# HGRN2 layer with MLP on one core: the MLP's first 512 hidden columns in seven block products, and half of one head's values kept on the chip

## The chip, the core and the metric

The kernel runs on one core of a Trainium2 chip. TensorE (PE in the profile) multiplies, PEld is its weight load, VectorE (DVE), ScalarE (ACT) and GpSimd (POOL) work on data in SBUF and PSUM, and SyncE (SP) issues most of the DMAs. The metric is the time of one execution on the device in microseconds (us), as a median of runs.

## The reference

One layer on x of 1024 rows (tokens) by 1024 columns, all in float32: a gated linear recurrence (HGRN2, 8 heads of 128), then an MLP with squared ReLU and 4096 hidden columns, each behind an RMS norm and added to x, and a last norm.

```python
h = _rmsnorm(x, norm_mix)
x = x + _hgrn2_mixer(h, w_in, lb, out_norm, w_out)   # q, f, i, g = split(h @ w_in); S_t = diag(f_t) S_{t-1} + k_t v_t^T
...                                                  # o = S_t^T q_t, normed, times silu(g), then o @ w_out
h = _rmsnorm(x, norm_mlp)
a = jax.nn.relu(h @ w1)                              # 1024x1024 by 1024x4096
x = x + (a * a) @ w2                                 # 1024x4096 by 4096x1024
return _rmsnorm(x, norm_final)
```

## The kernel before

**A product in three.** A float32 product is made of three matmuls in a faster format (fp32r). Each operand is split into a high part, a copy in that format that ACT makes (`AF.Copy`), and a low part, the rest, which DVE makes by a subtraction. `split_mm` (L222 to L225) then issues high by high, high by low and low by high. So each operand costs one pass of ACT and one of DVE.

**Seven products for eight.** Large products are done on 2 x 2 blocks with seven block products instead of eight (Winograd's form of Strassen's method). In the MLP a unit is 512 of the 4096 hidden columns; there are eight units. The blocks of the first product's activations are B11, B21 (first half of the 1024 rows) and B12, B22 (second half); their sums are t1 to t4. A unit's weights are four blocks a, b, c, d and the sums s1 to s4. The order of the seven (`SEQ`) is a on B11, s1 on t1, s2 on t2, s4 on B22, s3 on t3, b on B21, d on t4. Each is 24 matmuls of 128x512 into two PSUM banks of one of three sets (X, Y, Z); a set collects several block products, and `evac_1` moves what is needed into SBUF, adds, and applies ReLU and square.

**The stages in the trace.** Up to 424 us the heads' projections and scans; 424 to 528 the output projection (`proj_out`, PSUM name `op`), first for columns 0 to 511, then for 512 to 1023, with the scan of the last head (7) issued in units between its matmuls until about 466; from 528 the MLP's first product, unit 0 until 579, units 1 to 7 until about 820; then its second product and the last norm.

**Unit 0 before.** Unit 0 alone is a plain product, eight block products of 24 matmuls, 192 (`plain_mm`, PSUM names `pl`). x after the mixer is normed by row blocks of 128 (`hm`, `hn`, by `norm_scale`), transposed on PE eight times for each half of the rows (L206, PSUM name `tr`), copied with the norm's gain into `V` by ACT (L883), and split (`h1B`, L885 to L888). `transposes_2` makes such steps as a list of hooks; hooks of half 0 run in the output projection, those of half 1 between the matmuls of unit 0. `block_sums` (L96 to L104) later makes t1 to t4 out of `V`, in place, and `split_sum` (L115, L116) splits them into `ht`, for units 1 to 7.

**The order.** PE's order is written out by hand everywhere. In the output projection's second half and behind it, that of ACT, DVE, POOL and SP is the program's too; in the head stage these four are placed by a scheduler in order of priority. On each engine and queue instructions run in order, so what waits holds up what stands behind it.

**Values of the heads.** `zt` (L712 to L722) makes a head's output values, transposed, in two halves of 512 rows: DVE multiplies into `sg` (L718) and SP stores each half into `z_d` in DRAM (L721); only head 7's stay. `fetch` (L741) loads them again (`iz`, L747), and `split_value` (L736 to L738) splits them into `zh` for the output projection; in the same way it loads and splits the projection's weights (`iw` into `wo`). The table `LEFT` says which loads go with which block product of the last head; with its third last product, s3, goes head 6's first half, alone:

```python
LEFT = {"b": ("z", 0, range(last - 1), ("m0", "m1", "m8")), "s2": ("w", 0, range(4), ("hT07", "m9")),
        "s1": ("w", 0, range(4, last), ("m10", "m11")), "s3": ("z", 0, range(last - 1, last), ("m0",))}
```

In the scan of the last head, L397 and L403 make k and f for the next level, L390 q, L584 `qe`, and L590, L608 and L638 are PE's small matmuls for these levels (`lv`), whose results L568 to L572 copy under masks into `Ac`. L156 is the helper for additions, which adds the projection's result to x (`xr`) among others; L903 and its like store x into DRAM (`xd`).

Of the kernel before, what the change touches and what calls it, by code (L numbers as in the profile page):

```python
# [29 lines left out]
P = 128  # L30
D = 1024
# [18 lines left out]
def trunk(ctx: ExitStack, tc: tile.TileContext, x, gains, masks, gfin, w_in, w_out, w1, w2, out):  # L50
# [44 lines left out]
    def block_sums():  # L95

        for k in range(2):
            nc.vector.tensor_tensor(R[0, k], R[0, k], R[1, k], ALU.subtract)
        for k in range(2):
            nc.vector.tensor_tensor(R[1, k], R[1, 2 + k], R[1, k], ALU.subtract)  # L100
        for k in range(2):
            nc.vector.scalar_tensor_tensor(R[1, 2 + k], R[0, k], -1.0, R[1, 2 + k], op0=ALU.mult, op1=ALU.subtract)
        for k in range(2):
            nc.vector.scalar_tensor_tensor(R[0, 2 + k], R[1, 2 + k], -1.0, R[0, 2 + k], op0=ALU.mult, op1=ALU.subtract)  # L104

    def split_sum(n):
        half, k0 = SUMS[n]
# [155 lines left out]
    with tc.tile_pool(name="scan", bufs=1) as sp:  # L263
# [277 lines left out]
        def scan_units(h, tl):  # L541
# [168 lines left out]
            def zt():  # L710

                z = tl["sg"]  # L712
                for a in range(2):
# [6 lines left out]
                    if h < NH - 1:  # L720
                        nc.sync.dma_start(z_d[h][:, o], z[:, o])  # L721
# [18 lines left out]
        def fetch(what, half, heads_, places):  # L740

            for h0, m in zip(heads_[::2], places):
# [11 lines left out]
                "s1": ("w", 0, range(4, last), ("m10", "m11")), "s3": ("z", 0, range(last - 1, last), ("m0",))}  # L754
# [79 lines left out]
    def raw_tile(name):  # L834

        k = raw_no[0] % 9
        raw_no[0] += 1
        if k < 2:
            return mslot(k, [P, D], name)
        return slot((12, 13, 14, 8, 9, 10, 11)[k - 2], [P, D], name)  # L840
# [29 lines left out]
    load_w1(0, "abcd")  # L870
    hm = [slot(tb, [P, D], f"hm{tb}") for tb in range(4)]
    rs = {}
    junk = slot(14, [P, D], "junk")
    w0 = {}

    def transposes_2(half, hn):

        def one(kb):
            flat, g, t = transposed(1, half, kb, hn)
            if kb % 2 == 0:  # L880
                R[half, kb // 2] = slot((4, 8)[half] + kb // 2, [P, 2, 512], f"V{half}{kb}")
            r = R[half, kb // 2][:, kb % 2]
            nc.scalar.activation(r, flat, AF.Copy, scale=g)  # L883
            if kb % 2:
                nc.scalar.activation(t[:, 0], r, AF.Copy)  # L885
            else:
                nc.vector.tensor_copy(t[:, 0], r)
            nc.vector.tensor_tensor(t[:, 1], r, t[:, 0].bitcast(F32), ALU.subtract)  # L888
        return [lambda kb=kb: one(kb) for kb in range(KB)]

    def norm_first(tb):
        nc.sync.dma_start(x1[tb], xs[tb])
        rs[tb] = norm_stats(xs[tb], 8 + tb, hm[tb])
        if tb in (1, 2):
            norm_scale(hm[tb - 1], xs[tb - 1], rs[tb - 1], True)
        if tb == 3:
            norm_scale(hm[2], xs[2], rs[2])
            w0["a"] = split_w(raw["a", 0], "wa0")
            norm_scale(hm[3], xs[3], rs[3])
            w0["b"] = split_w(raw["b", 0], "wb0")  # L900

    def norm_second(tb):
        nc.sync.dma_start(x1[tb], xs[tb])  # L903
        rs[tb] = norm_stats(xs[tb], 8 + tb, junk)
        for _ in range((0, 2, 3, 3)[tb - 4]):
            hook()

    order_all(E.SP)
    proj_out(A, 1, range(NH), norm_first)
    hooks += transposes_2(0, hm)  # L910
    proj_out(B, 1, range(NH), norm_second)
    while hooks:
        hook()
    hn = [slot(tb - 4, [P, D], f"hn{tb}") for tb in B]
    for tb in B:
        norm_scale(hn[tb - 4], xs[tb], rs[tb], tb % 2)


    def act_tile(n, u):
        return slot({"e11": u % 2, "e22": 2, "e12": 3, "e21": 4 if u else 13, "t1": 5, "t2": 6, "t4": 7}[n], [P, 2, 512], f"{n}{u}")  # L920

    def square(t):
        nc.scalar.activation(t, t, AF.Square)  # L923

    def relu_square(t, sign=1.0):
        nc.scalar.activation(t, t, AF.Relu, scale=sign)  # L926
        square(t)

    def store(n, u, t):
        nc.sync.dma_start(act_d[n, u], t)  # L930

    def combos_1(u, e):

        t1 = e["t1"] = act_tile("t1", u)
        nc.vector.tensor_tensor(t1, e["e11"], e["e12"], ALU.subtract)
        store("t1", u, t1)
        nc.vector.tensor_tensor(e["e12"], e["e22"], e["e12"], ALU.subtract)
        store("t3", u, e["e12"])
        t2 = e["t2"] = act_tile("t2", u)
        nc.vector.scalar_tensor_tensor(t2, t1, -1.0, e["e22"], op0=ALU.mult, op1=ALU.subtract)  # L940
        store("t2", u, t2)

    def combos_2(u, e):
        t4 = act_tile("t4", u)
        nc.vector.scalar_tensor_tensor(t4, e["t2"], -1.0, e["e21"], op0=ALU.mult, op1=ALU.subtract)
        store("t4", u, t4)

    def plain_mm(i, half):

        pss = [psum.tile([P, 512], F32, name=f"pl{i}{half}{p}", tag="d") for p in range(2)]  # L950
        for k in range(2):
            w = w0["abcd"[2 * i + k]]
            for p in range(2):
                for kb in range(4):
                    o = slice((4 * p + kb) * P, (4 * p + kb + 1) * P)
                    t = hc[("B11", "B21", "B12", "B22")[2 * half + k], kb]
                    if k:
                        hook()
                    split_mm(pss[p], w[0][:, o], w[1][:, o], t[:, 0], t[:, 1], (k, kb) == (0, 0), (k, kb) == (1, 3))
        return pss  # L960

    def plain_out(e, n, pss):
        t = e[n] = act_tile(n, 0)
        for p in range(2):
            nc.scalar.activation(t[:, p], pss[p], AF.Relu)
        square(t)

    e0 = {}
    hooks += transposes_2(1, hn)
    w0["c"] = split_w(raw["c", 0], "wc0")  # L970
    hooks.insert(4, lambda: w0.update(d=split_w(raw["d", 0], "wd0")))
    c11 = plain_mm(0, 0)
    while hooks:
        hook()
    plain_out(e0, "e11", c11)
    c21 = plain_mm(1, 0)
    load_w1(1, "acdb")
    block_sums()
    plain_out(e0, "e21", c21)
    c12 = plain_mm(0, 1)  # L980
    c22 = plain_mm(1, 1)
    split_sum("t3")
    split_sum("t1")
    split_sum("t2")
# [5 lines left out]
    first_2 = (NU - 1) * NS  # L990
# [38 lines left out]

    prep(0)  # L1030
    plain_out(e0, "e12", c12)
    prep(1)
    prep(2)
    plain_out(e0, "e22", c22)
    split_sum("t4")
    for n in ("e11", "e21", "e22"):
        store("B" + n[1:], 0, e0[n])

    def evac_1(u, m, e, ps):
# [6 lines left out]
        elif m == "d":  # L1046
            t = e["e21"] = act_tile("e21", u)
            for p in range(2):
                nc.scalar.activation(t[:, p], ps[p], AF.Relu, scale=-1.0)
            square(t)  # L1050
            store("B21", u, t)
            combos_1(u, e)
            combos_2(u, e)
        else:
            t = e[{"s4": "e12", "s3": "e22", "b": "e11"}[m]]
            for p in range(2):
                nc.vector.tensor_tensor(t[:, p], t[:, p], ps[p], ALU.add)  # L1057
            relu_square(t, -1.0 if m == "s3" else 1.0)
            if m == "s3":
                store("B22", u, t)  # L1060
            if m == "b":
                store("B11", u, t)
# [51 lines left out]
    def product_2(k, pb, s, first, last_):  # L1114
        hi, lo = sides[k]
        w = ws[k]
        for p in range(2):
            o, t = slice(512 * p, 512 * p + 512), slice(P * pb, P * pb + P)
            split_mm(banks[s][pb], hi[:, p, t], lo[:, p, t], w[0][:, o], w[1][:, o], first and p == 0,
                     last_ and p == 1, skip_group_check=True)  # L1120

    banks, e = {}, {}
    for k, (which, u, v, s, m, n) in enumerate(steps):
        first = m in ("a", "s1", "b")
        ending = which == 2 and u >= 4
        if first and v == 0:
            banks[s] = [psum.tile([P, 512], F32, name=f"m{which}{s}{u}{p}", tag=BANK[s]) for p in range(2 * which)]
        load_act(k + LOOK + 2)
        if which == 1:
            w = ws.pop(k)  # L1130
            for p in range(2):
                for kb in range(4):
                    o = slice((4 * p + kb) * P, (4 * p + kb + 1) * P)
                    t = hc[n, kb]
                    split_mm(banks[s][p], w[0][:, o], w[1][:, o], t[:, 0], t[:, 1], first and kb == 0, kb == 3,
                             skip_group_check=True)
            if u + 1 < NU and m in ("s2", "s4"):
# [84 lines left out]
```

## Time and profile before

| | |
|---|---|
| median of 3 runs | 1156.57 us (1155.76 to 1157.57) |
| the profiled execution | 1156.81 us |
| its span, first to last instruction | 1155.0 us |
| granted PE clock, mean | 0.998 of full speed |
| PE busy | 1138.8 us, 99%, 7106 instructions |
| DVE busy | 789.9 us, 68%, 1140 |
| ACT busy | 577.7 us, 50%, 1008 |

Busy times are of the profiled execution. PE's is near the span, so the kernel's time is the work that PE is given and the few microseconds in which PE waits. A row of a timeline has the start and the duration in us, then engine, line, operation and tiles (output, then inputs), and in brackets how long the engine was idle before and what released it. Neighbouring rows on PE overlap, since matmuls are pipelined.

### The profile page before, as it was taken

What the parts mean: (1) busy time and instruction counts of PE and PEld (TensorE: products, weight loads), DVE (VectorE), ACT (ScalarE), POOL (GpSimd) and SP (SyncE); (2) the same over time, 40 slices, a digit from 0 to 9 for tenths busy, and PEclk for the clock granted to TensorE, in tenths of its full rate; (3) what the DMA queues carried; (4) which work ended last, traced back from release to release, by engine and by line L of the source; (5) the groups of instructions that cost most, each with busy time, mean ns of one, the idle gap of its engine ahead of it and who ended that gap; (6) DMA issues with size and microseconds to landing.
All of it is one profiled execution on the core that took longest, in us unless ns stands there. A gap on an engine that the chain in (4) does not pass through costs nothing.

```text
span 1155.0 us, 17539 instructions
## 1 busy us (share of the span) xinstructions
PE 1138.8 (99%) x7106; PEld 941.4 (82%) x7106; DVE 789.9 (68%) x1140; ACT 577.7 (50%) x1008; POOL 38.6 (3%) x67
## 2 busy tenths in 40 slices
PE   8999999999999999999999999999999999999997
PEld 7778888787878878888888888888888888888886
DVE  6997878768687775436756654665487756677673
ACT  7656556474655663237544554454453443323552
POOL 1000000000000000010000000000000000000011
PEclk9999999999999999999999999999999999999999
DMA  7112111111121274121245324542797545322331
GB/s 260 37 38 74 56 37 56 56 38 56 57 64 47 83 264 129 37 91 55 91 164 201 147 90 164 200 163 84 278 368 288 191 159 191 137 91 92 128 128 74
DMA packets 43138, 143.38 MB, mean 124 GB/s; under 512 B 4912, under 2 KB 5040, under 8 KB 43056
## 3 DMA queue, kind: packets, MB, share of 16 engines
q1 hardware_dynamic: 42192, 141.05, 34.5%
q8 instruction: 56, 0.92, 0.3%
q10 hardware_dynamic: 864, 1.20, 0.3%
q14 instruction: 26, 0.21, 0.1%
HBM read 100.81 MB, written 41.42 MB: 123 GB/s over the span
## 4 chain that ended last, share of the span: by engine, by line
PE 87%; DVE 8%; ACT 2%; DMA 1%; issue 1%; POOL 0%; SPq 0%; POOLq 0%; DVEq 0%; ACTq 0%
PE m2X L224 5%; PE m2X L223 5%; PE m2X L225 5%; PE m1X L225 4%; PE m1X L223 4%; PE m1X L224 4%; PE pX L223 3%; PE pX L225 3%; PE pX L224 3%; PE m2Y L224 3%; PE m2Y L225 3%; PE m2Y L223 3%; PE op L223 2%; PE op L225 2%; PE op L224 2%; PE m1Y L225 2%
## 5 line engine op out<-in xcount | busy, mean ns | idle before, releaser
L1023 ACT ACTIVATE a<-ai 128x1024 fp32r<-128x1024 f32 x56 | 59.0, 1053 | 71.5 <-PE m2X L224 24.5
L1024 DVE TENSOR_TENSOR a<-ai,a 128x1024 fp32r<-128x1024 f32 x56 | 68.2, 1218 | 11.5 <-ACT a L1023 11.5
L926 ACT ACTIVATE e<-e 128x1024 f32<-128x1024 f32 x21 | 22.3, 1062 | 67.3 <-DVE e L1057 67.3
L223 PE MATMUL op<-wo,zh 128*128 128x512 f32 x128 | 51.0, 399 | 0.0
L225 PE MATMUL op<-wo,zh 128*128 128x512 f32 x128 | 50.0, 391 | 0.0
L224 PE MATMUL op<-wo,zh 128*128 128x512 f32 x128 | 49.8, 389 | 0.0
L156 DVE TENSOR_TENSOR xr<-xr,op 128x512 f32<-128x512 f32 x24 | 16.4, 686 | 44.9 <-PE op L225 44.9
L1084 DVE TENSOR_TENSOR acc<-acc,m2X 128x512 f32<-128x512 f32 x32 | 21.1, 684 | 35.7 <-PE m2X L225 35.6
L390 DVE TENSOR_TENSOR q<-q,f 128x512 f32<-128x512 f32 x56 | 38.4, 686 | 2.1 <-PE lv L638 2.0
L397 DVE TENSOR_TENSOR k<-k,f 128x512 f32<-128x512 f32 x56 | 38.2, 683 | 0.0
L923 ACT ACTIVATE e<-e 128x1024 f32<-128x1024 f32 x32 | 34.0, 1062 | 1.0
L615 ACT ACTIVATE AT<-Ac 32x256 f32<-32x256 f32 x32 | 13.3, 415 | 37.8 <-DVE Ac L611 32.8
L156 DVE TENSOR_TENSOR raw<-raw,raw 128x512 f32<-128x512 f32 x42 | 28.9, 687 | 0.8
L225 PEld LDWEIGHTS op<-wo,zh 128*128 128x128 f32 x128 | 24.0, 188 | 5.2
L224 PEld LDWEIGHTS op<-wo,zh 128*128 128x128 f32 x128 | 24.1, 188 | 4.7
L223 PEld LDWEIGHTS op<-wo,zh 128*128 128x128 f32 x128 | 24.0, 188 | 4.8
L1045 ACT ACTIVATE e<-m1X 128x512 f32<-128x512 f32 x28 | 16.0, 592 | 19.9 <-PE m1X L225 19.9
L707 ACT ACTIVATE z<-o,rs_z 128x128 f32<-128x128 f32 x64 | 17.4, 384 | 16.3 <-POOL rs_z L126 16.3
L695 PE MATMUL o<-v,AT 128*128 128x128 f32 x128 | 23.4, 275 | 0.0
L697 PE MATMUL o<-S,q 128*128 128x128 f32 x112 | 21.7, 275 | 0.0
L1084 DVE TENSOR_TENSOR acc<-acc,m2Y 128x512 f32<-128x512 f32 x16 | 10.8, 685 | 15.4 <-PE m2Y L225 13.2
L125 POOL TENSOR_SCALAR rs_f<-fs 128x1 f32<-128x1 f32 x4 | 2.0, 512 | 577.7 <-ACT ot L1088 577.7
(1726 smaller groups left out, 3712.9 us busy)
## 6 DMA issues: line engine op xcount, KB each, us to landing
raw<-in_w_in SPq DMA_DIRECT2D x32, 512.0 KB, 3.7
ai<-adt SPq DMA_DIRECT2D x32, 512.0 KB, 4.5
adB<-e SPq DMA_DIRECT2D x24, 512.0 KB, 2.6
adt<-t SPq DMA_DIRECT2D x24, 512.0 KB, 4.3
ai<-adB SPq DMA_DIRECT2D x24, 512.0 KB, 4.5
x<-in_x SPq DMA_DIRECT2D x8, 512.0 KB, 7.2
iw<-in_w_out SPq DMA_DIRECT2D x16, 256.0 KB, 3.4
xr<-in_x SPq DMA_DIRECT2D x8, 512.0 KB, 6.7
```

The source lines that it names most:

```text
L156: nc.vector.tensor_tensor(out_, a, b, ALU.add)
L223: nc.tensor.matmul(ps, lhi, rhi, start=start, stop=False, **more)
L224: nc.tensor.matmul(ps, lhi, rlo, start=False, stop=False, **more)
L225: nc.tensor.matmul(ps, llo, rhi, start=False, stop=stop, **more)
L390: nc.vector.tensor_tensor(qo, qo, te.to_broadcast([P, n, m]), ALU.mult)
L397: nc.vector.tensor_tensor(ke, ke, to.to_broadcast([P, n, m]), ALU.mult)
L695: nc.tensor.matmul(ps[:, j, :], AT[:, c, :], v[:, c, :], start=True, stop=c == 0)
L923: nc.scalar.activation(t, t, AF.Square)
L926: nc.scalar.activation(t, t, AF.Relu, scale=sign)
L1023: nc.scalar.activation(hi, x, AF.Copy)
L1024: nc.vector.tensor_tensor(lo, x, hi.bitcast(F32), ALU.subtract)
L1084: nc.vector.tensor_tensor(t, t, ps, op)
```

## The change

Two things are changed.

**Unit 0 in seven block products.** `plain_mm`, `plain_out` and `block_sums` go; unit 0 joins the list of steps of units 1 to 7 with an order of its own: a on B11, b on B21, s1 on t1, s2 on t2, s3 on t3, s4 on B22, then unit 1's a, then d on t4. It has 168 matmuls. Its weights need seven splits and four sums, made by `prep`, which stands partly in the norm stage; t1 to t4 are made one by one by `sums`, the transposes of half 1 run in the last part of the first block product and in the second, and the splits of B22 come behind the third, those of B12 go. What follows each product on ACT, DVE and SP is listed in `behind_0`. Unit 1's weights are loaded at other points, the places of raw weights are given by a new table, and unit 0's results go through copies and additions out of PSUM, as those of the other units, in place of a ReLU straight out of PSUM.

**Head 6, first half.** Its values are split where `zt` makes them; the store into DRAM, the load, and the entry "s3" of `LEFT` go. The second half of head 6 is stored and loaded as before.

```diff
-    def block_sums():
...
+    def split_sum(n, at=None):
+        half, k0 = at or SUMS[n]
...
-                    if h < NH - 1:
+                    if (h, a) == (last - 1, 0):
+                        t = zh[0, h] = place("z", 0, h)
+                        split_value(t, z[:, o])
+                    elif h < last:
                         nc.sync.dma_start(z_d[h][:, o], z[:, o])
...
-                "s1": ("w", 0, range(4, last), ("m10", "m11")), "s3": ("z", 0, range(last - 1, last), ("m0",))}
+                "s1": ("w", 0, range(4, last), ("m10", "m11"))}
...
-        k = raw_no[0] % 9
+        k = raw_no[0]
         raw_no[0] += 1
...
+        place = ("m0", "m1", 12, 13, 14, "m0", 10, 11, 8, 9)[k] if k < 10 \
+            else ("m1", 13, "m0", 10, 9, 12, 14, 11, 8)[(k - 10) % 9]
...
-    def plain_mm(i, half):
...
-    c11 = plain_mm(0, 0)
...
-    plain_out(e0, "e11", c11)
-    c21 = plain_mm(1, 0)
-    load_w1(1, "acdb")
-    block_sums()
...
     steps = [(1, u, 0, *s) for u in range(1, NU) for s in SEQ]
+    steps[:1] = [(1, 0, 0, *SEQ[i]) for i in (0, 5, 1, 2, 4, 3)] + [steps[0], (1, 0, 0, *SEQ[6])]
...
+    def split_block(half, kb):
+        name = BLOCKS[half][kb // 4]
+        r = R[half, kb // 2][:, kb % 2]
+        t = hc[name, kb % 4] = hslot(half, kb, f"h1{name}{kb}")
+        if half or kb % 2:
+            nc.scalar.activation(t[:, 0], r, AF.Copy)
+        else:
+            nc.vector.tensor_copy(t[:, 0], r)
+        nc.vector.tensor_tensor(t[:, 1], r, t[:, 0].bitcast(F32), ALU.subtract)
+
+    def sums(n, ks=range(2)):
+        for k in ks:
+            a, b, c, d = R[0, k], R[0, 2 + k], R[1, k], R[1, 2 + k]
+            if n == "t1":
+                nc.vector.tensor_tensor(a, a, c, ALU.subtract)
...
+        if tb == 3:
+            norm_scale(hm[2], xs[2], rs[2])
+            prep(0)
+            norm_scale(hm[3], xs[3], rs[3])
+            prep(1)
...
+        if tb == 4:
+            prep(2)
+        for _ in range((3, 3, 2, 0)[tb - 4]):
+            hook()
+        if tb == 7:
+            prep(3)
...
+        if tb == 7:
+            prep(4)
+            load_w1(1, "a")
...
+    def adds_1(m, e, ps):
+        t = e[ADDED[m]]
+        for p in range(2):
+            nc.vector.tensor_tensor(t[:, p], t[:, p], ps[p], ALU.add)
...
+    behind_0 = {
+        1: (lambda: sums("t2"), split_5, lambda: evac_0("a"), lambda: split_sum("t2", t1_at)),
+        2: (lambda: sums("t3"), lambda: split_sum("t3")),
+        3: (lambda: copy_0(0), lambda: [split_block(1, kb) for kb in range(4, 8)], lambda: copy_0(1), lambda: evac_0("s1")),
+        4: (lambda: prep(6), lambda: sums("t4"), lambda: split_sum("t4")),
...
+    hooks += [lambda: None] + tr[:4] + [lambda: (sums("t1", (0,)), block_sum(raw, "s4", 0), sums("t1", (1,)), tr[4]()), tr[5], lambda: (split_sum("t1"), tr[6]()), tr[7]]
     for k, (which, u, v, s, m, n) in enumerate(steps):
...
+                    if k == 1 or (k, p) == (0, 1) and kb > 1:
+                        hook()
```

What moves is shown by the engines' orders; line numbers of the changed file are 11 lower up to L718 (now L707) and 8 lower behind it (L738 is L730). DVE where head 6's values are made, before: the two halves of the values, `sg6`, between weight splits.

```order
L738 TENSOR_TENSOR wo02_4433<-iw02_4430,wo02_4433 128x512
L718 SCALAR_TENSOR_TENSOR sg6_3904<-zt60_4406,gz_166,sg6_3904 128x512
L718 SCALAR_TENSOR_TENSOR sg6_3904<-zt61_4413,gz_166,sg6_3904 128x512
L738 TENSOR_TENSOR wo00_4424<-iw00_4421,wo00_4424 128x512
L738 TENSOR_TENSOR wo01_4427<-iw00_4421,wo01_4427 128x512
```

Changed:

```order
L707 SCALAR_TENSOR_TENSOR sg6_3904<-zt60_4406,gz_166,sg6_3904 128x512
L707 SCALAR_TENSOR_TENSOR sg6_3904<-zt61_4415,gz_166,sg6_3904 128x512
L730 TENSOR_TENSOR wo00_4426<-iw00_4423,wo00_4426 128x512
L730 TENSOR_TENSOR zh06_4412<-sg6_3904,zh06_4412 128x512
L730 TENSOR_TENSOR wo01_4429<-iw00_4423,wo01_4429 128x512
```

The low half of `zh06`, head 6's first half, now stands between two weight splits, three instructions behind the values. DVE some ten instructions later, in front of k of the last head's scan, before (`zh10` and `zh11` are values of heads 0 and 1, second half; `e17` and `sg7` belong to the gate of head 7; `Ac` is a level's scores):

```order
L738 TENSOR_TENSOR zh10_4827<-iz10_4824,zh10_4827 128x512
L446 TENSOR_TENSOR sg7_4481<-sig07_4482,e17_4452 128x512
L738 TENSOR_TENSOR zh11_4830<-iz10_4824,zh11_4830 128x512
L568 COPY_PREDICATED Ac_153<-mk_74,lv7_0_0_4499 128x128
L738 TENSOR_TENSOR zh06_4487<-iz06_4485,zh06_4487 128x512
L397 TENSOR_TENSOR k7_4216<-k7_4216,f7_4217 128x512
L569 COPY_PREDICATED Ac_153<-mk_74,lv7_0_0_4499 128x64
```

Changed:

```order
L730 TENSOR_TENSOR zh10_4824<-iz10_4821,zh10_4824 128x512
L435 TENSOR_TENSOR sg7_4483<-sig07_4484,e17_4454 128x512
L730 TENSOR_TENSOR zh11_4827<-iz10_4821,zh11_4827 128x512
L557 COPY_PREDICATED Ac_153<-mk_74,lv7_0_0_4496 128x128
L730 TENSOR_TENSOR zh12_4833<-iz12_4830,zh12_4833 128x512
L386 TENSOR_TENSOR k7_4216<-k7_4216,f7_4217 128x512
L558 COPY_PREDICATED Ac_153<-mk_74,lv7_0_0_4496 128x64
```

In front of k stands the low half of `zh12` (head 2, second half) where that of `zh06` stood. ACT at the start of the MLP, before: copies of half 1's transposes into `V`, the splits of B12 and B22 (`h1B`) between them, a weight split, then the ReLU of unit 0's first result.

```order
L883 ACTIVATE V12_5598<-tr113_5605,gn_73 128x512
L885 ACTIVATE h1B123_5610<-V12_5598 128x512
L854 ACTIVATE wd0h_5617<-ud0_5176 128x1024
L883 ACTIVATE V14_5630<-tr114_5624,gn_73 128x512
L883 ACTIVATE V14_5630<-tr115_5637,gn_73 128x512
L885 ACTIVATE h1B225_5642<-V14_5630 128x512
L883 ACTIVATE V16_5655<-tr116_5649,gn_73 128x512
L883 ACTIVATE V16_5655<-tr117_5662,gn_73 128x512
L885 ACTIVATE h1B227_5667<-V16_5655 128x512
L965 ACTIVATE e110_5671<-pl000_5541 128x512
L965 ACTIVATE e110_5671<-pl001_5542 128x512
```

Changed:

```order
L924 ACTIVATE V14_5623<-tr114_5618,gn_73 128x512
L924 ACTIVATE V14_5623<-tr115_5628,gn_73 128x512
L104 ACTIVATE ht10_5637<-V00_5366 128x512
L104 ACTIVATE ht11_5640<-V00_5366 128x512
L104 ACTIVATE ht12_5643<-V02_5385 128x512
L104 ACTIVATE ht13_5646<-V02_5385 128x512
L924 ACTIVATE V16_5654<-tr116_5649,gn_73 128x512
L924 ACTIVATE V16_5654<-tr117_5659,gn_73 128x512
L848 ACTIVATE ws40h_5673<-uc0_5171 128x1024
L1022 ACTIVATE e110_5677<-m1X00_5552 128x512
L1022 ACTIVATE e110_5677<-m1X01_5553 128x512
```

The four high halves of t1 (`ht10` to `ht13`) stand in front of the copies of the last two transposes, the splits of B22 are gone from here, and the first result is taken out of PSUM by copies.

## Rows read from the trace of the kernel before

**Rows 1.** The page's part 1: busy us, share of the span, instructions.

```profile
PE 1138.8 (99%) x7106; PEld 941.4 (82%) x7106; DVE 789.9 (68%) x1140; ACT 577.7 (50%) x1008; POOL 38.6 (3%) x67
```

**Rows 2.** The waits of PE: us in total, times, longest us.

```profile
PE lv L590 <- DVE qe L584: 2.6, 1, 2.6
PE lv L638 <- DVE k L397: 1.7, 5, 0.7
```

**Rows 3.** Windows: us, busy us by engine (instructions), PEclk, DMA share, GB/s.

```profile
534.00:545.60 11.60, 11.54 (x67) 9.48 (x66) 9.53 (x16) 10.61 (x17) 0.00 (x0) 1.00 0.01 1
545.60:578.00 32.40, 32.40 (x144) 26.85 (x143) 24.24 (x27) 17.40 (x27) 0.00 (x0) 1.00 0.25 81
...
sum 76.00, PE 75.94 PEld 62.81 DVE 51.42 ACT 42.93 POOL 0.00; mean PE 25.32 PEld 20.94 DVE 17.14 ACT 14.31 POOL 0.00
```

**Rows 4.** Timeline of PE, 426 to 439: start, duration, line, operation, idle.

```profile
426.63 0.39 PE L225 MATMUL op<-wo,zh 128*128 128x512 f32 x1
429.64 0.89 PE L590 MATMUL lv<-qe,k 128*32 128x48 f32 x64 [2.62 <-DVE qe L584]
...
437.63 0.46 PE L638 MATMUL lv<-q,k 128*32 128x32 f32 x32 [0.36 <-DVE k L397]
```

**Rows 5.** The chain of waits from 412 to 425: start us, us, what.

```profile
414.37 4.26 DMA zd<-sg
...
418.64 4.61 DMA iz<-zd
...
423.28 0.64 ACT zh L737
```

**Rows 6.** Timeline of DVE, 418 to 430.

```profile
421.11 0.29 DVE L568 COPY_PREDICATED Ac<-mk,lv 128x128 f32<-128x128 uint8 x1
423.94 0.69 DVE L738 TENSOR_TENSOR zh<-iz,zh 128x512 fp32r<-128x512 f32 x1 [2.54 <-ACT zh L737]
424.55 0.69 DVE L397 TENSOR_TENSOR k<-k,f 128x512 f32<-128x512 f32 x1
...
428.81 0.68 DVE L584 TENSOR_TENSOR qe<-q,f 128x512 f32<-128x512 f32 x1
```

**Rows 7.** Timeline of ACT, 412 to 424.

```profile
416.23 0.65 ACT L515 ACTIVATE e<-pY 128x512 f32<-128x512 f32 x1
...
419.77 0.62 ACT L737 ACTIVATE zh<-iz 128x512 fp32r<-128x512 f32 x1
```

**Rows 8.** Groups by line, 545 to 570: busy us, mean ns, idle.

```profile
L116 DVE TENSOR_TENSOR ht<-V,ht 128x512 fp32r<-128x512 f32 x12 | 7.3, 682 | 2.0 <-ACT ht L115 2.0
L115 ACT ACTIVATE ht<-V 128x512 fp32r<-128x512 f32 x12 | 6.3, 616 | 0.0
```

**Rows 9.** Timeline of PE, 534 to 538.

```profile
534.66 0.87 PE L206 MATMUL tr<-ident,hn 128*128 128x128 f32 x4
535.29 0.48 PE L223 MATMUL pl<-h1B,wb0h 128*128 128x512 f32 x1
...
536.07 0.60 PE L206 MATMUL tr<-ident,hn 128*128 128x128 f32 x4
536.43 0.47 PE L223 MATMUL pl<-h1B,wb0h 128*128 128x512 f32 x1
```

**Rows 10.** Timeline of all engines, 527 to 530.

```profile
527.85 1.48 PE L206 MATMUL tr<-ident,hm 128*128 128x128 f32 x12
528.05 0.69 DVE L156 TENSOR_TENSOR xr<-xr,op 128x512 f32<-128x512 f32 x1 [1.31 <-PE op L225]
528.77 0.32 SPq L903 DMA_DIRECT2D xd<-xr  x1
```

**Rows 11.** Timeline of all engines, 534 to 538.

```profile
534.98 1.04 ACT L854 ACTIVATE wc0h<-uc 128x1024 fp32r<-128x1024 f32 x1
...
536.05 1.23 DVE L855 TENSOR_TENSOR wc0l<-uc,wc0h 128x1024 fp32r<-128x1024 f32 x1 [1.01 <-ACT wc0h L854]
```

**Rows 12.** DMA issues, 520 to 600: KB each, median us to landing.

```profile
xd<-xr SPq DMA_DIRECT2D x2, 512.0 KB, 2.7
```

More of the change, by code (lines that the diff above doesn't have):

```diff
@@ L867, in block_sum @@
         return r["c" if m in ("s1", "s2", "s4") else m, u]
[L870 to L946, printed above, removed]
-    def plain_mm(i, half):
[L950 to L960, printed above, removed]
@@ L1028, in prep, with transposes_2, one @@
             load_w2({"s2": "a", "s4": "c", "d": "d", "b": "b"}[m], u + 4)
[L1030 to L1037, printed above, removed]
+    load_w1(0, "abcd")
+    hm = [slot(tb, [P, D], f"hm{tb}") for tb in range(4)]
+    rs = {}
+    junk = slot(11, [P, D], "junk")
+    def transposes_2(half, hn):
+        def one(kb):
+            ps = transpose_bank(1, half, kb)
+            transpose_rows(ps, hn, kb, range(4))
+            if kb % 2 == 0:
+                R[half, kb // 2] = slot((4, 8)[half] + kb // 2, [P, 2, 512], f"V{half}{kb}")
+            r = R[half, kb // 2][:, kb % 2]
+            nc.scalar.activation(r, ps.rearrange("p a b -> p (a b)"), AF.Copy, scale=gn[:, 1, kb:kb + 1])
+            if half == 0:
+                split_block(half, kb)
+        return [lambda kb=kb: one(kb) for kb in range(KB)]
@@ new lines, in split_block @@
+    def split_block(half, kb):
+        name = BLOCKS[half][kb // 4]
+        r = R[half, kb // 2][:, kb % 2]
+        t = hc[name, kb % 4] = hslot(half, kb, f"h1{name}{kb}")
[9 more added lines that the diff above has]
+                nc.vector.tensor_tensor(a, a, c, ALU.subtract)
+            elif n == "t3":
+                nc.vector.tensor_tensor(c, d, c, ALU.subtract)
+            elif n == "t2":
+                nc.vector.scalar_tensor_tensor(a, a, -1.0, d, op0=ALU.mult, op1=ALU.subtract)
+            else:
+                nc.vector.scalar_tensor_tensor(b, a, -1.0, b, op0=ALU.mult, op1=ALU.subtract)
@@ new lines, in trunk, with act_tile, square, relu_square @@
+    order_all(E.SP)
+    proj_out(A, 1, range(NH), norm_first)
+    hooks += transposes_2(0, hm)
+    hn = []
+    proj_out(B, 1, range(NH), norm_second)
+    def act_tile(n, u):
+        return slot({"e11": u % 2, "e22": 2 if u else 14, "e12": 3 if u else 12, "e21": 4, "t1": 5, "t2": 6, "t4": 7}[n], [P, 2, 512], f"{n}{u}")
+    def square(t):
+        nc.scalar.activation(t, t, AF.Square)
+    def relu_square(t, sign=1.0):
+        nc.scalar.activation(t, t, AF.Relu, scale=sign)
+        square(t)
@@ new lines, in store, with combos_1 @@
+    def store(n, u, t):
+        nc.sync.dma_start(act_d[n, u], t)
+    def combos_1(u, e):
+        t1 = e["t1"] = act_tile("t1", u)
+        nc.vector.tensor_tensor(t1, e["e11"], e["e12"], ALU.subtract)
+        store("t1", u, t1)
+        nc.vector.tensor_tensor(e["e12"], e["e22"], e["e12"], ALU.subtract)
+        store("t3", u, e["e12"])
+        t2 = e["t2"] = act_tile("t2", u)
+        nc.vector.scalar_tensor_tensor(t2, t1, -1.0, e["e22"], op0=ALU.mult, op1=ALU.subtract)
+        store("t2", u, t2)
@@ L1039, in evac_1, with combos_2 @@
+    def combos_2(u, e):
+        t4 = act_tile("t4", u)
+        nc.vector.scalar_tensor_tensor(t4, e["t2"], -1.0, e["e21"], op0=ALU.mult, op1=ALU.subtract)
+        store("t4", u, t4)
     def evac_1(u, m, e, ps):
@@ L1051, in evac_1, with squares_1 @@
             store("B21", u, t)
-            combos_1(u, e)
-            combos_2(u, e)
-        else:
[L1055 to L1062, printed above, removed]
+            if u:
+                combos_1(u, e)
+                combos_2(u, e)
+        else:
+            adds_1(m, e, ps)
+            squares_1(u, m, e)
+    ADDED = {"s4": "e12", "s3": "e22", "b": "e11"}
+    def adds_1(m, e, ps):
+        t = e[ADDED[m]]
+        for p in range(2):
+            nc.vector.tensor_tensor(t[:, p], t[:, p], ps[p], ALU.add)
+    def squares_1(u, m, e):
+        t = e[ADDED[m]]
+        relu_square(t, -1.0 if m == "s3" else 1.0)
+        if m == "s3":
+            store("B22", u, t)
+        if m == "b":
+            store("B11", u, t)
     acc = {}
@@ L1126, in trunk @@
         if first and v == 0:
-            banks[s] = [psum.tile([P, 512], F32, name=f"m{which}{s}{u}{p}", tag=BANK[s]) for p in range(2 * which)]
+            banks[s, u if which == 1 else 0] = [psum.tile([P, 512], F32, name=f"m{which}{s}{u}{p}", tag=BANK[s]) for p in range(2 * which)]
         load_act(k + LOOK + 2)
@@ L1172, in trunk @@
             for pb in range(4):
-                evac_2(m, pb, banks[s][pb])
+                evac_2(m, pb, banks[s, 0][pb])
         if ending and m == "b" and v < 2:
```

88 lines of the change are left out of this document (48 added, 40 removed).

## Prediction

> **What bounds the kernel now.** First the busy shares: TensorE (PE) is busy for 1138.8 of 1155.0 us [rows 1], so what it issues is the time, and the other engines count only where PE waits for them. So the table of PE's waits comes next [rows 2]: the longest is 2.6 us, at the matmuls of L590 (scan of the last head), which wait for VectorE (DVE); L638 waits five times for the same engine, 1.7 us in all. Then the stages that the change touches. In the MLP's first product the window of 545.6 to 578 shows 144 matmuls in 32.40 us, PE busy for all of it at a granted clock of 1.00, the 2.4 GHz level [rows 3]: nothing is idle. DVE has 51.42 and ScalarE (ACT) 42.93 us of work in the 76 us of the last row, so both have room on average.
>
> **Part 1: fewer matmuls.** Unit 0 goes from eight block products to seven. A block product is 2 x 4 groups of three matmuls, 24, so 192 become 168, all of 128x512. Which duration to use is a choice: a matmul's own row says 0.39 us [rows 4], but matmuls overlap, so what one costs is the mean distance of starts, 32.40 / 144 = 0.225 us [rows 3]. 24 x 0.225 = 5.40 us saved. The 64 transposes of the MLP's input stay.
>
> The page "TensorE: Matmul & The Clock Gate" of the Trainium skill, section "Back-to-back issue gap", gives 131 ns for each matmul of 512 columns in a sustained stream of loads and matmuls. By that the saving would be an estimated 3.1 us; the trace disagrees, with 144 in 32.40 us.
>
> **Part 2: half of head 6's values no longer pass through DRAM.** The chain of waits shows the way before: a 256 KB store, 4.26 us, then the load of the same data, 4.61 us, then ACT's half of the split at 423.28 [rows 5]. DVE works in order, and its half of that split (423.94) stands ahead of L397 (k, 424.55): DVE is idle for 2.54 us before the one, and everything from the other to L584 (qe, 428.81 to 429.49) comes late by as much [rows 6]. L590 waits for qe, 2.62 us, until 429.64 [rows 4].
>
> After, that split sits some 8 us earlier, among the weight splits behind the two instructions of L718, and costs DVE 0.61 us there (the step from 423.94 to 424.55). What follows moves by it: L568 from 421.11 to 421.72. In the old split's place stands zh12, whose load was issued far earlier and whose ACT half follows zh11's. That one is at 419.77 [rows 7]; with the delay of 0.6 it starts at 420.4, zh12's a step on (12 of L115 in 6.3 us [rows 8], 0.53), and ends 0.62 later, at 421.5. So zh12 starts on DVE when L568 is done: 0.29 of its row less the 0.08 by which neighbours overlap (0.69 against the step of 0.61), at 421.93. k follows at 422.54 instead of 424.55: 2.01 us earlier. From k to qe DVE has no idle time, so qe moves with it, and L590's wait shrinks from 2.62 to 0.61; DVE's own work is what is late next there. Bounds: 1.4 if a further step of 0.61 lands ahead of k; the whole 2.62 and the 0.36 of L638 at 437.63 [rows 4], 2.98, if holes take up more. I take 2.01, which is put together from steps of the rows alone.
>
> ACT's extra half (0.53) stands ahead of the copy at 416.23 [rows 7], which frees a PSUM bank for PE; if PE starts its next product later by part of that, it reaches L590 later, where it still waits: no cost. On SP's queue six loads of x stood behind the load that waited at 418.64; they go earlier, and are used 40 us later: no gain.
>
> The page "DMA: Bandwidth & Descriptors" of the Trainium skill, section "Anatomy of one DMA — SWDGE (gpsimd) path", would price such a store and load at an estimated 2.6 us each, so that the values would land before DVE wants them and nothing would be gained. The trace decides: 4.26 and 4.61 us, and an idle DVE [rows 5, 6].
>
> **Part 3: the first transposes of rows 512 to 1023.** Before, the first bank of them takes 0.63 us until the next product starts, a later one 0.36 [rows 9]: 0.27 of waiting for the last row block's norm (hn7). After, 21 matmuls go ahead of them, from 527.85 (when the last 12 transposes of the other half started [rows 10]): 21 x 0.225 = 4.7, so hn7 is wanted at 532.6. The last sum of x ends at 528.74 [rows 10]. Behind it come, on DVE, a weight sum, priced as the 1024-wide pass of 1.23 [rows 11], to 529.9; on ACT the high half of that weight, 1.04, and hn7, a pass of the same width: 531.9 to 532.0. Cover 0.6 us, so the 0.27 goes. If not, 0.
>
> **Part 4: what is added beside PE.** Three more weight splits (ACT 1.04, DVE 1.23 each [rows 11]), four weight sums (1.23), six additions out of PSUM (0.69, as the sum at 528.05 [rows 10]); less four value splits (0.6) and four casts (0.4). DVE +3.7 + 4.9 + 4.1 - 2.4 - 1.6 = +8.7, less what the old order had in idle steps, about a microsecond: +7 to +9. ACT +3.1, and +3.1 for three more 1024-wide passes. DVE's 51.42 becomes about 59 of some 70 us [rows 3]: it fits on average, so I cost it at nothing. Where it stands decides:
> - Third block product (s1 on t1). Its PSUM bank is free when ACT has copied the transposes two before it, and in ACT's order four splits of t1 stand ahead of that copy. Banks of transposes come every 1.14 us (535.29 to 536.43 [rows 9]): the sixth starts at 532.6 + 5 x 1.14 = 538.3 and is full 0.6 later (the row of 536.07), at 538.9; a copy and four splits at 0.53 and the copy wanted, 0.6, end at 542.15. PE is there at 532.6 + 7 x 1.14 + 0.36 + 6 x 0.225 = 542.3. Cover 0.15: cost 0 to 0.5, I take 0.
> - t1 itself: two sums (1.23 each) and four low halves 0.61 apart (12 in 7.3 us [rows 8]). On DVE the low half of ws30 goes ahead of them, into the tile that x's last block is stored from; the store is issued at 528.77 and lands 2.7 us later [rows 10, 12], 531.5, before DVE comes to it, at 532 or later.
> - t2 is wanted 24 x 0.225 = 5.4 us after t1 and asks for two sums and four low halves, 2.5 + 2.4 = 4.9: cover 0.5, and what DVE is ahead by. No cost.
>
> **Sum.** -5.40 - 2.01 - 0.27 = -7.68. The profiled run took 1156.81 us, 1.8 more than its span, and lies 0.24 above the median of the runs shown. 1156.81 - 7.68 = 1149.1, or 1148.9 beside the median: I say 1149.0.
>
> **The rivals.** A measurement of this kernel can tell about 0.2%, 2.3 us, from no change: 1154.3 to 1158.9 is the same.
> - A. The wait only moves. DVE is full from k on; if L590's wait keeps its size (another value split stops ahead of k, or L638 takes over), only Parts 1 and 3 are gained: 1156.81 - 5.67 = 1151.1. For it: DVE ends both kinds of PE's waits [rows 2]. Against it: the idle 2.54 us end with data from DRAM that are no longer fetched [rows 5, 6]. 0.16.
> - B. The front of unit 0 waits. If the splits of t1 and of t2 each come late by the two sums ahead of them, 2 x 2.46 = 4.9 of the 7.68 go: 1154.0. For it: the cover of 0.15. Against it: with each later product the covers grow. 0.08.
> - C. Slower. The added vector and scalar work is exposed: from the transposes to the fourth product DVE and ACT wait for each other, and all of 8 + 3.1 + 3.1 = 14.2 us becomes waits of PE: 1156.81 + 14.2 - 7.7 = 1163.3. It starts once the work in arrears at the third product exceeds its cover of 0.15 us, and decides for slower from 10 us of new waits on (7.7 and the 2.3 that can be told). For it: in the 11.6 us of the transposes ACT is already busy for 10.61 [rows 3]. Against it: four value splits of half 1 leave just that stretch, and go behind the third product. 0.07.
> - D. A matmul taken away frees less than its step of 0.225 us, because some 40% of the step is its weight load's and goes to a neighbour: 24 x 0.13 = 3.1, so 1156.81 - 3.1 - 2.3 = 1151.4 (the rate is that of the page of the Trainium skill in Part 1). Against it: with PE busy for the whole of that window a step has nothing else in it [rows 3]. 0.03.
> - Mine, 0.66, with its own range from its terms' bounds: the least 5.40 + 1.4 + 0 - 0.5 = 6.3, the most 5.40 + 2.98 + 0.27 = 8.65, so 1148.2 to 1150.5.
>
> **How the numbers follow.** Faster by over 0.2%: mine, A and D, and half of B: 0.66 + 0.16 + 0.03 + 0.04 = 0.89. Same: the other half of B and 0.01 of C, 0.05. Slower: the rest of C, 0.06. The range takes in mine, A, D and B with one late split (1149.1 + 2.46 = 1151.6) and ends 0.8 beyond it, at 1152.4; its low end, 1147.0, is my least of 1148.2, less the 0.24 to the median, and the 0.8 by which the lowest of the runs shown lies under it. 0.8 is also what I add above.
>
> **What would show it.** PE has 24 matmuls fewer. The wait of 2.62 us at the scan's matmuls (L590, whose line number will differ) is 0.4 to 0.9; one of 2 or more is A. No load of head 6's first half stands in the chain around 420, and DVE has no idle time of 2.5 us ahead of k. The first transposes of rows 512 to 1023 take the time of later ones. At the third and fourth products of unit 0 PE's waits stay under 0.5 us; 2 us for DVE or ACT there is B, and PE busy for less than 85% from 530 to 575 is C. If the rows come out as said and the time is still outside 1148.2 to 1150.5, a price is wrong, that of a matmul above all.

## The result and the profile after

The changed kernel took 1148.82 us, the median of 4 runs (1148.8 to 1148.92); before, in the same comparison, 1156.16 us (1154.98 to 1157.57, 4 runs). The ratio is 0.9936, with a 95% interval of 0.9919 to 0.9953: faster by 0.5 to 0.8%. The profiled run took 1148.80, 8.0 us less than that of before. In a second comparison it was 1149.0 (5 runs) beside 1157.55 (9 runs), a ratio of 0.9926 [0.9914, 0.9939].

The page of the changed kernel, its part 1 for PE (busy us, share, instructions), to be set beside [rows 1], and PE's waits (us in total, times, longest), beside [rows 2]:

```profile
PE 1133.5 (99%) x7082; PEld 936.8 (82%) x7082; DVE 797.2 (70%) x1145; ACT 583.7 (51%) x1014; POOL 37.9 (3%) x67
```

```profile
PE lv L627 <- DVE k L386: 2.1, 7, 0.7
...
PE lv L579 <- DVE qe L573: 0.2, 1, 0.2
```

24 matmuls are gone, and the 2.62 us ahead of the scan's matmuls (L590 before, L579 now) are 0.24. The waits of L627, L638 before, rose from 1.7 to 2.1 us over all heads; the one in the last head, behind L579, stayed at 0.4. The timeline of PE around the place, for [rows 4]:

```profile
426.84 0.39 PE L214 MATMUL op<-wo,zh 128*128 128x512 f32 x1
427.47 0.89 PE L579 MATMUL lv<-qe,k 128*32 128x48 f32 x64 [0.24 <-DVE qe L573]
...
435.43 0.46 PE L627 MATMUL lv<-q,k 128*32 128x32 f32 x32 [0.37 <-DVE k L386]
```

L579 starts at 427.47 instead of 429.64, 2.17 us earlier, and the 0.37 at 435.43 is what it was. DVE ahead of it, for [rows 6], and ACT, for [rows 7]:

```profile
415.36 0.69 DVE L730 TENSOR_TENSOR zh<-sg,zh 128x512 fp32r<-128x512 f32 x1
...
421.57 0.29 DVE L557 COPY_PREDICATED Ac<-mk,lv 128x128 f32<-128x128 uint8 x1
421.76 0.68 DVE L730 TENSOR_TENSOR zh<-iz,zh 128x512 fp32r<-128x512 f32 x1
422.37 0.69 DVE L386 TENSOR_TENSOR k<-k,f 128x512 f32<-128x512 f32 x1
...
426.64 0.68 DVE L573 TENSOR_TENSOR qe<-q,f 128x512 f32<-128x512 f32 x1
```

```profile
416.61 0.64 ACT L504 ACTIVATE e<-pY 128x512 f32<-128x512 f32 x1
...
420.23 1.14 ACT L729 ACTIVATE zh<-iz 128x512 fp32r<-128x512 f32 x2
```

The low half of head 6's values stands at 415.36, among the weights; behind L557 (L568 before) comes zh12 with no idle time, and k starts at 422.37 instead of 424.55. ACT made the two halves that DVE wanted one behind the other, from 420.23.

At the start of the MLP, PE's matmuls on the transposed rows 512 to 1023, for [rows 9]; the first row is unit 0's first matmul:

```profile
527.01 0.39 PE L212 MATMUL m1X<-h1B,wa0h 128*128 128x512 f32 x1
...
531.78 0.60 PE L195 MATMUL tr<-ident,hn 128*128 128x128 f32 x4
...
532.92 0.60 PE L195 MATMUL tr<-ident,hn 128*128 128x128 f32 x4
...
534.05 0.60 PE L195 MATMUL tr<-ident,hn 128*128 128x128 f32 x4
```

The three banks are 1.14 and 1.13 us apart: the first is no longer slower than the others. All engines behind the last sum of x, for [rows 10, 11]: the sum, the store, the high half of ws20, and hn7 on ACT.

```profile
527.22 0.69 DVE L145 TENSOR_TENSOR xr<-xr,op 128x512 f32<-128x512 f32 x1 [0.19 <-PE op L214]
...
527.93 0.32 SPq L964 DMA_DIRECT2D xd<-xr  x1
...
529.12 1.06 ACT L848 ACTIVATE ws20h<-uc 128x1024 fp32r<-128x1024 f32 x1
...
530.09 1.16 ACT L184 ACTIVATE hn<-xr,rs_n 128x1024 f32<-128x1024 f32 x1
```

hn7 is ready at 531.25, 0.5 us before the first of these transposes starts at 531.78. The windows, for [rows 3], from the transposes on (us, then busy us of PE, PEld, DVE, ACT, POOL, the granted clock, DMA share, GB/s):

```profile
530.90:542.50 11.60, 11.60 (x68) 9.59 (x67) 8.44 (x10) 9.15 (x15) 0.00 (x0) 1.00 0.09 32
...
sum 71.10, PE 71.10 PEld 58.87 DVE 52.27 ACT 45.59 POOL 0.00; mean PE 23.70 PEld 19.62 DVE 17.42 ACT 15.20 POOL 0.00
```

PE has no idle time, though DVE now has 52 and ACT 46 us in 71. One row of each kernel measures the change up to a common point, the first matmul of unit 1 on t2; first before, then after:

```profile
587.56 0.39 PE L223 MATMUL m1X<-ht,ws21h 128*128 128x512 f32 x1
```

```profile
579.70 0.39 PE L212 MATMUL m1X<-ht,ws21h 128*128 128x512 f32 x1
```

7.86 us earlier. The last matmul of all, 1147.65 before and 1139.79 after, is 7.86 earlier too, so everything was gained before that point and nothing given back behind it.

### The profile page after: what moved, and what is told of

Its sections match the earlier page's. It is cut to its first block, busy times and chain, and to the rows that moved or that the text cites. A ratio compares the mean times of both kernels' runs of the same rounds, so it can differ in the third digit from the quotient of the medians.

```text
span 1147.0 us, 17503 instructions
## 1 busy us (share of the span) xinstructions
PE 1133.5 (99%) x7082; PEld 936.8 (82%) x7082; DVE 797.2 (70%) x1145; ACT 583.7 (51%) x1014; POOL 37.9 (3%) x67
## 4 chain that ended last, share of the span: by engine, by line
PE 86%; DVE 10%; ACT 1%; issue 1%; DMA 1%; POOL 0%; POOLq 0%; DVEq 0%; ACTq 0%
PE m2X L214 5%; PE m1X L213 5%; PE m2X L212 5%; PE m1X L212 5%; PE m1X L214 5%; PE m2X L213 5%; PE pX L212 3%; PE pX L214 3%; PE pX L213 3%; PE m1Y L212 3%; PE m1Y L213 3%; PE m2Y L214 3%; PE m2Y L212 3%; PE m1Y L214 3%; PE m2Y L213 3%; PE op L212 2%
## 5 line engine op out<-in xcount | busy, mean ns | idle before, releaser
L994 ACT ACTIVATE e<-e 128x1024 f32<-128x1024 f32 x24 | 25.5, 1062 | 72.5 <-DVE e L1041 72.5
L991 ACT ACTIVATE e<-e 128x1024 f32<-128x1024 f32 x32 | 34.0, 1062 | 1.0
L690 ACT ACTIVATE z<-o 128x128 f32<-128x128 f32 x64 | 16.8, 282 | 8.9 <-PE o L686 8.6
```

## The experiments

**Each part alone.** The kernel before with the second part only:

```diff
-                    if h < NH - 1:
+                    if (h, a) == (last - 1, 0):
+                        t = zh[0, h] = place("z", 0, h)
+                        split_value(t, z[:, o])
+                    elif h < last:
                         nc.sync.dma_start(z_d[h][:, o], z[:, o])
...
-                "s1": ("w", 0, range(4, last), ("m10", "m11")), "s3": ("z", 0, range(last - 1, last), ("m0",))}
+                "s1": ("w", 0, range(4, last), ("m10", "m11"))}
```

> The kernel before with only the second part: the first half of head 6's values split where it is made, unit 0 still in eight block products. Theory (the parts add, the wait really goes): the wait of L590 falls from 2.62 to about 0.3 us, as in the changed kernel, and the time is 2.0 to 2.3 us below that of before (about 1154.0 to 1154.5). Rival A (the wait only moves): no gain beyond 0.5 us, and a wait of 2 us or more stands at L590 or at another group of the scan. Rival (the parts need each other): a gain that differs from 2.1 by 1 us or more.

Measured: 1154.63 us (1154.43 to 1154.85, 11 runs) beside 1156.42 of before (1154.21 to 1159.36, 15 runs): 1.8 us less, ratio 0.9985 [0.9976, 0.9995]. Its wait of PE, with the old line number:

```profile
PE lv L590 <- DVE qe L584: 0.2, 1, 0.2
```

The wait went and did not move on (L638 waits for 0.37 us behind it, 0.36 before), so rival A falls. The size is 0.2 below the range that was expected, and the interval is wide, because the runs of before spread over 5 us and these over 0.4.

The changed kernel with the store and the load put back (the same lines, the other way):

> The changed kernel with head 6's values stored and loaded again as before: only unit 0 in seven block products. Theory: 24 matmuls at 0.2265 us and 0.3 us of the first transposes' wait, 5.4 to 5.8 us below before (about 1150.4 to 1151.0), with the wait of 2.6 us back at the scan's matmuls. Rival D (a matmul is worth 0.13 us): 3.1 to 3.5 below. Rival (the parts need each other): other than 5.6 by 1 us or more.

Measured: 1151.63 us (1149.2 to 1151.96, 5 runs), 4.8 below the same 1156.42, ratio 0.9963 [0.995, 0.9975]: less than the theory's number by 0.6 to 1.0, and again a spread of 2.8 us. The profiled run was the one of 1149.2, where PE waited for 0.66 us only, since the load took 2.94 us (chain of waits; start, duration, what):

```profile
414.35 3.95 DMA zd<-sg
...
418.32 2.94 DMA iz<-zd
```

The medians are too unsteady here to tell 5.6 from 4.8. What they show is that both kernels with the transfer spread, and both without it don't. So the steady pair prices unit 0 better: the kernel with the second part alone (1154.63) and the changed kernel (1148.82 and 1149.0), neither of which waits for the transfer, lie 5.6 to 5.8 us apart, where 5.40 + 0.27 was said.

**The kernel before, twice more.**

> The kernel before once more, for the length of the store and load of head 6's values and the wait of L590 behind them, which seem to differ from run to run (the runs of before spread over 5 us, those of the kernels without the transfer over 0.4). Theory: the wait of L590 and the time go together, the time being 1154.4 plus what the wait has beyond 0.24 us, less a few tenths. Rival (the spread has another place): the wait is again about 2.6 us whatever the time.

> As the run before it, one more look at the kernel before: the wait of L590 again goes with the time by the theory, and stays at about 2.6 us by the rival.

The first took 1155.27 us. Its chain of waits and its wait at L590:

```profile
414.42 3.92 DMA zd<-sg
...
418.36 3.37 DMA iz<-zd
```

```profile
PE lv L590 <- DVE qe L584: 1.0, 1, 1.0
```

The second took 1158.21 us:

```profile
414.20 4.61 DMA zd<-sg
...
418.83 4.80 DMA iz<-zd
```

```profile
PE lv L590 <- DVE qe L584: 3.2, 1, 3.2
```

Store and load took 3.92 + 3.37 us in the one and 4.61 + 4.80 in the other, against 4.26 + 4.61 in [rows 5]; the wait was 1.0, 3.2 and 2.6. Store and load less the wait is 6.2 to 6.3 us in all three, and in the profiled run with unit 0 alone (3.95 + 2.94, and 0.66): what the transfer takes beyond that, PE waits. Taking 1154.6 (the median of the part alone, with 0.24 of wait; the expectation took its profiled run, 1154.4) as the base, the theory gives 1155.4 and 1157.6 for the two, measured 1155.27 and 1158.21. So of the 2.94 us between the two executions 2.2 are the wait.

The second execution has 0.6 us more than the theory gives, and its trace shows a place for them. The timeline of PE behind the long wait, and one of the windows behind it (us, busy us of PE, the granted clock, DMA share, GB/s):

```profile
430.03 0.89 PE L590 MATMUL lv<-qe,k 128*32 128x48 f32 x64 [3.17 <-DVE qe L584]
430.85 0.65 PE L223 MATMUL op<-wo,zh 128*128 128x512 f32 x1
...
434.83 0.40 PE L224 MATMUL op<-wo,zh 128*128 128x512 f32 x1
```

```profile
432.00:433.00 1.00, 1.00 (x3) 0.50 0.56 205
```

After PE had stood for 3.17 us its granted clock fell to 0.50, the lower of its two levels (1.2 GHz), until about 434.3. The ten matmuls from 430.85 to 434.83 took 3.98 us; in the profile of before, where PE had stood for 2.62 us and the granted clock stayed at 1.00, the same ten took 2.41 (430.46 to 432.87). Some of these 1.6 us come back, since L638 no longer waits. So here the wait cost more than its own length. Of the 33 runs of before that stand beside the experiments nine have a mean granted clock of 0.997 or less, and all nine took 1156.97 us or more; every run of the changed kernel has 0.998 or 0.999. So the clock has a share in the spread; how large was not measured. Why the transfer's length varies was not tried.

**The transfer without its reader.** The changed kernel, with the store and the load made and the split not taken from them:

```diff
                         split_value(t, z[:, o])
-                    elif h < last:
+                    if h < last:
...
                 for h in two:
+                    if (what, half, h) == ("z", 0, last - 1):
+                        continue
...
-                "s1": ("w", 0, range(4, last), ("m10", "m11"))}
+                "s1": ("w", 0, range(4, last), ("m10", "m11")), "s3": ("z", 0, range(last - 1, last), ("m0",))}
```

> The changed kernel, but the first half of head 6's values is also stored in DRAM and loaded again into the same place as before, with nothing reading it; VectorE's order is that of the changed kernel. Theory (the gain is that VectorE's queue no longer stops for the load): the time stays within 0.3 us of the changed kernel, and the wait at the scan's matmuls stays about 0.24 us. Rival (the gain is the traffic taken away, or SP's queue and the slot m0 that come free earlier): it falls back by 1 to 2 us.

Measured: 1149.18 us (1149.11 to 1150.09, 5 runs), 0.2 to 0.4 above the changed kernel (1149.0 and 1148.82). The waits of PE:

```profile
PE lv L627 <- DVE k L386: 3.5, 9, 1.3
...
PE lv L579 <- DVE qe L573: 0.2, 1, 0.2
```

L579 waits as briefly as in the changed kernel, with all the traffic back: the gain is DVE's queue that no longer stops, not the bytes. But in the profiled run, the one of 1150.09, L627 waited 3.5 us in total, 1.3 at once, because the next load came late (chain of waits):

```profile
425.18 8.07 DMA iz<-zd
...
433.27 1.26 ACT zh L729 x2
```

That load, of two other heads' values, takes the tile that the needless load held; it was issued behind it and took 8.07 us. So there is a small second effect of the transfer, on the load behind it: this run took 1.1 to 1.3 us more than the changed kernel. The other four, of which there is no profile, took 0.1 to 0.4 more.

**The price of a matmul.** The changed kernel with 24 matmuls left out, 12 in each of two units:

```diff
-                for kb in range(4):
+                for kb in (0, 3) if (u, m) in ((3, "b"), (5, "b")) else range(4):
```

> The changed kernel without 24 more matmuls of 128x512: in the products of b on B21 of units 3 and 5 the middle two of four groups in each bank are left out (that part of the sum is missing); nothing else moves. Theory: 24 x 0.2265 = 5.4 us below the changed kernel, about 1143.4. Rival D (a matmul taken away frees 0.13 us): 3.1 below. Rival (the other engines are as late as PE): less than 3, with new waits of PE at the products behind.

Measured: 1144.4 us (1144.29 to 1144.56, 4 runs), 4.4 to 4.6 below the changed kernel: neither the theory's 5.4 nor the rival's 3.1. The timeline shows where the rest is, at unit 4's product on t2, some 18 us behind the first gap (all engines):

```profile
690.84 1.23 DVE L849 TENSOR_TENSOR ws24l<-uc,ws24h 128x1024 fp32r<-128x1024 f32 x1 [1.13 <-ACT ws24h L848]
...
691.34 0.50 PE L212 MATMUL m1X<-ht,ws24h 128*128 128x512 f32 x1
...
691.68 0.40 PE L213 MATMUL m1X<-ht,ws24h 128*128 128x512 f32 x1
...
692.12 0.19 PEld L214 LDWEIGHTS m1X<-ht,ws24l 128*128 128x128 f32 x1 [0.48 <-DVE ws24l L849]
```

PE's weight load waits 0.48 us for the low half of ws24, which DVE ends at 692.07; the same stands at the next unit but one, 766. Three matmuls take 1.11 us at each place (691.34 to 692.45) instead of 0.68 (3 x 0.2265, the step in the rows of the changed kernel), so 2 x 0.43 of the 5.44 us are lost and 4.6 are left, as measured. PE came 2.72 us earlier (12 x 0.2265), and had a cover of only 2.3 there. To test that, the same 24 in four portions of six:

```diff
-                for kb in range(4):
+                for kb in (0, 2, 3) if m == "b" and u in (2, 3, 4, 5) else range(4):
```

> The changed kernel without 24 matmuls of 128x512 once more, but six from each of four units (2 to 5), in the product of b on B21 (that part of the sum is missing): PE gets ahead by 1.36 us a unit instead of 2.72. Theory (the 0.48 us that PE waited for ws24l in the run with 12 left out at a time came from being ahead by more than the cover of 2.72 - 0.46 = 2.3 us at the s2 product of the next unit): no such wait, and 5.4 us below the changed kernel of the same call. Rival (a matmul taken away frees only 4.5 / 24 = 0.19 us): 4.5 below.

> The changed kernel itself, on the same chip as the run beside it: 1148.8 to 1149.2 us by every theory.

Measured: 1143.53 us (1143.5 to 1143.82, 4 runs) and 1149.0 (1148.93 to 1149.09, 5 runs) beside it: 5.47 less, 0.228 a matmul, and no wait of PE from 590 to 830. The theory holds, the rivals fall. A matmul taken away is worth its step, as long as the weights keep ahead.

**The narrowest cover of unit 0.** Two passes of ACT more, first ahead of the last copies of the transposes, then behind the splits of t2 (the lines are cut to the place that changes):

```diff
-    lambda: (split_sum("t1"), tr[6]())
+    lambda: (split_sum("t1"), [nc.scalar.activation(raw["s3", 0], R[0, 2].rearrange("p a b -> p (a b)"), AF.Copy) for _ in range(2)], tr[6]())
...
-            lambda: split_sum("t2", t1_at)),
+            lambda: split_sum("t2", t1_at), lambda: [nc.scalar.activation(raw["s3", 0], R[0, 2].rearrange("p a b -> p (a b)"), AF.Copy) for _ in range(2)]),
```

> The changed kernel with two more passes of ScalarE over 1024 columns (a copy that nothing reads) between the four splits of t1 and the copies of the last two banks of transposes, ahead of unit 0's third product. Theory (that product's PSUM bank waits for those copies, with a cover of about 0.2 us): two passes of some 0.95 us by the distance of starts, so PE waits 1.9 - 0.2 = 1.7 us there and the time is 1.4 to 1.9 us above the changed kernel. Rival (the cover is larger than the rows say, or another engine ends the wait): under 0.5 us.

Measured: 1151.19 us (1150.88 to 1152.75, 5 runs), 2.2 to 2.4 above the changed kernel (1149.0 and 1148.82), more than the 1.4 to 1.9 expected. PE's only wait from 526 to 600, and PE's last and first matmul of the two products:

```profile
PE m1Y L212 <- ACT V L924: 1.8, 1, 1.8
```

```profile
541.72 0.40 PE L214 MATMUL m1Z<-h1B,wb0l 128*128 128x512 f32 x1
543.93 0.50 PE L212 MATMUL m1Y<-ht,ws10h 128*128 128x512 f32 x1 [1.81 <-ACT V L924]
```

The wait is where it was said, for the copy of a transposed bank by ACT. The 1.8 us count from the end of a matmul's row, which overlaps its neighbour; by the starts, 541.72 to 543.93, PE loses 2.21 - 0.23 = 1.98 us. The two passes held ACT for 2.04 (from 541.16 to 543.20), so the cover was under 0.1. The rest of the 2.2 to 2.4 stands ahead of the passes: ACT's splits of t1 start at 539.08 here, at 538.67 and 538.90 in the two profiles of the changed kernel. The changed kernel's own rows at that place, ACT's copies behind the four splits, PE's last and first matmul of two products and its weight load between them:

```profile
538.67 2.18 ACT L104 ACTIVATE ht<-V 128x512 fp32r<-128x512 f32 x4
540.75 1.25 ACT L924 ACTIVATE V<-tr,gn 128x512 f32<-128x512 f32 x2
```

```profile
541.31 0.40 PE L214 MATMUL m1Z<-h1B,wb0l 128*128 128x512 f32 x1
541.48 0.19 PEld L212 LDWEIGHTS m1Y<-ht,ws10h 128*128 128x128 f32 x1 [0.21 <-ACT V L924]
541.54 0.44 PE L212 MATMUL m1Y<-ht,ws10h 128*128 128x512 f32 x1
```

The copy that frees the bank ends at about 541.4. PE's weight load already waits 0.21 us for it, and its matmul still starts at 541.54, one step of 0.23 behind the last: the cover is all but used up.

> The same two passes of ScalarE, but behind the splits of t2, where ScalarE is idle for 2.9 us in the changed kernel. Theory: hidden, the time within 0.2 us of the changed kernel. Rival C (ScalarE's and VectorE's added work has no room in unit 0): 1 us or more above.

Measured: 1149.09 us (1148.85 to 1149.33, 5 runs), no more than 0.3 from the changed kernel: hidden, as the timeline of ACT shows, where the idle time ahead of the next splits shrinks from 2.86 to 0.76:

```profile
546.15 2.16 ACT L1135 ACTIVATE us<-V 128x1024 f32<-128x1024 f32 x2
549.07 2.29 ACT L104 ACTIVATE ht<-V 128x512 fp32r<-128x512 f32 x4 [0.76 <-DVE V L946]
```

So the same work costs 2 us at the one place and nothing 5 us later. Rival C would have needed both to show.

## Why the prediction was right

Forecast 1149.0, measured 1148.82; on the profiles, a gain of 7.68 forecast and 7.86 to 8.0 seen. By the medians the gain is 7.3 us in the first comparison and 8.6 in the second, since that of before moves; that the forecast is met to 0.2 us is in part luck. By its steps:

- **Part 1, -5.40.** Right. Twice 24 more matmuls were left out, and where the weights kept ahead it gave 5.47. Rival D (0.13 us a matmul) is out, and with it the 131 ns of the Trainium skill's "TensorE: Matmul & The Clock Gate", section "Back-to-back issue gap", for this stream of matmuls.
- **Part 2, -2.01.** Right in its mechanism and on the two profiles: k came 2.18 us earlier, L590's successor 2.17, and PE's wait is 0.24 where 0.61 was said, because DVE and ACT in front of it came 0.17 earlier, and PE was itself later by 0.21. But the term was taken as fixed, with bounds of 1.4 to 2.98. The profiles of the kernels with the transfer put the wait at 0.7, 1.0, 2.6 and 3.2 us, so what the change takes away is 0.4 to 3.0, and the profile of before happened to lie near the middle. Over many runs the median is 1.8. That the profile lay there is luck. The lower bound should have reached to 0.4, which one profile can't show, and that a long wait can also lower PE's granted clock (the second execution of before above) was in no term. The page "DMA: Bandwidth & Descriptors" of the Trainium skill, by which nothing would be gained, gives its figure for transfers that GpSimd issues; these are issued by SyncE, and the shortest of the chains with a reader, 3.95 + 2.94 us, still makes PE wait.
- **Part 3, -0.27.** The 0.27 went, as the rows show; no experiment took it alone. The working had two errors. The wait before was for a norm made by DVE (the weight load waits 0.29 us for L197, whose last row ends at 535.04), hn6 and not hn7; ACT's hn7 ended only 0.04 us later, so the sum is the same. The other cancelled by luck. The prediction counted the 21 matmuls from 527.85, where before the last 12 transposes of the other half start. These do not go away: in the changed kernel they stand inside the output projection, so unit 0 starts 1.23 us later by that clock (its first matmul is at 527.01, 2.07 earlier than the 529.08 of before, behind those transposes), and the last sum of x is moved by them as well: it is at 527.22, and 528.05 less 2.07 would be 525.98. Both ends of the cover moved by about the same, 0.6 was said and 0.5 measured.
- **Part 4, 0.** Right, though narrowly. The cover of 0.15 us at the third product was under 0.1 by the two passes put in, and a weight load waited 0.21 us there; no matmul waited from 526 to 600. That the waits at t2, the splits and the loads would cost nothing holds too. The added work came out as counted: DVE is busy for 7.3 us more (+7 to +9 was said), ACT for 6.0 (+6.2).
- **Rivals.** A is out by the second part alone, B and C by PE's full windows, D by the matmuls left out. B was near: another 0.1 us of ACT's work ahead of that copy would have begun to show.

What was not foreseen is the steadiness: the changed kernel's runs lie within 0.2 us in each comparison, those of before within 2.6 in the first and 5 in all.

## What to carry to other kernels

Where an in-order engine has an instruction that waits for a DMA, what stands behind it inherits the DMA's variance; a profile shows one draw, so bound such a wait by several profiles, or by the shortest and the longest transfer in them. Where PE is full, price a matmul by the distance of starts, and check at each later product whether the weights and the PSUM copies stay ahead once PE comes earlier: the gain stops where the cover does. Work added to a half idle engine is free or not by its place in the order, not by the engine's share.

## What was not expected of the hardware

The same 256 KB store and load took 3.92 + 3.37, 4.26 + 4.61 and 4.61 + 4.80 us in three executions of one program, and set most of the difference between their times. After a wait of 3.17 us PE's granted clock stood at 0.50 for some 3 us, and ten matmuls took 3.98 us instead of 2.41. And when PE was 2.72 us early it lost 0.43 us to a weight split that had never shown in a wait.
